# A hybrid S5 and mLSTM layer with a gated FFN: the first half of the output projection's features is summed in other PSUM banks than the second, in blocks 1 to 3

## The chip, the cores and the metric

The kernel runs on one core of one Trainium2 chip. The metric is the device time of one execution in microseconds (us), lower being better. Three runs of the kernel before took 2789.68, 2792.05 and 2795.96 us; the median is 2792.05 us. Every time below is in us unless it is marked otherwise. The engines are called as the profile calls them: PE (TensorE, matrix products), DVE (VectorE), ACT (ScalarE), POOL (GpSimd) and SP (SyncE, which issues the DMA transfers).

## The reference

One layer of a sequence model works on 16 meta tokens and 2048 tokens (L = 2064) of width 1024 in float32. The token mixer runs two branches, a state-space model (`y_a`) and a chunked mLSTM (`y_b`), gates and merges them, projects the sum with `w_out`, and adds the normed result to its input. The channel mixer is a convolutional gated FFN of width 2816. The part around the change is this:

```python
merged = (jax.nn.sigmoid(ga) * (y_a.astype(dtype) @ w_a)
          + jax.nn.sigmoid(gb) * (y_b.astype(dtype) @ w_b))
h1 = x + rmsnorm(merged @ w_out, g_post)                       # end of the token mixer

h2 = rmsnorm(h1, g_pre)                                        # channel mixer
a = causal_dwconv(h2 @ w_gate, w_conv, b_conv)
out = h1 + rmsnorm((gelu(a) * (h2 @ w_up)) @ w_down, g_post2)
```

The kernel returns the 2048 rows behind the meta tokens.

## The kernel before, in words

**How a product is made.** Every float32 operand is split in two parts, a high part (a copy in the float32r format) and a low part (what is left). A product of two matrices is then three passes of PE into one PSUM bank: high by high, high by low, low by high (`mm3`, lines 171 to 174). So each pass has its own line: L172 needs the two high parts, L173 the low part `wl` of the second operand (in the output projection, of the weights), L174 the low part of the first. Weights are split when they have landed: `split_w` (L153 to L160) lets ACT write the high part `wh` (L156) and DVE then the low part `wl` (L158, with a scale L160). The pool that holds `ws` (the weights as loaded), `wh` and `wl` is `dw`, with two buffers of each.

**PSUM.** The eight banks are three rings: `PS_BUFS = {"mm": 2, "ac": 4, "tp": 2}` (L33). `pst(tag, shape)` takes the next bank of a ring, and the first matmul into it waits until whoever read that bank last is done.

**The loop around the change.** The tokens of the mixer's last part are worked in four blocks of about 512 (four tiles of 128 rows; one block has a tile of 2 rows besides). For b = 0 to 3 the loop calls:

- `branches(b)`: for eight groups of features it multiplies both branches by their weights (results in `mm` and `ac`), DVE gates them with the loaded `gat` tiles (L978, L982, L983), and the merged sum is split into `mh` and `ml` (ACT L985, DVE L986).
- `front_a(b+1)` and `front_b(b+1)`: the first prepares the next block's state-space output without PE. The second loads the next block's mLSTM output as `yt` (L882); PE transposes it through the `tp` banks (L885), DVE gates it (L955) with a loaded `ot`, and it is split (ACT L956, DVE L957). In the last turn two `norm_block` calls stand here instead: rows of `h1` are loaded (L124), normed (ACT L135, DVE L105, POOL L107, DVE L137), transposed through `tp` (PE L148), multiplied by a gain out of the bank (DVE L150), and written to `h2` (L151), which the FFN reads.
- `out_post(b-1, i)` for the tiles of the block before: norm of the projected rows (ACT L1029, DVE L1031 and L105, POOL L107 for the power of minus one half, giving `rs`), DVE L1039 (multiply by `rs` and gain) and L1040 (add the input `xh`, loaded by L1037 into three buffers), and the write of `h1` (L1041).
- `out_proj(b)`: lines 992 to 1020, the changed function. For each half `nh` of the 1024 output features it takes one bank per token tile, loads the weights two k steps at a time (L1003; so four pairs make up a half), splits each pair, multiplies, and then copies the banks out to `o0` tiles (ACT L1016; DVE L1014 for two tiles of the very last half).
- `glu(b+1)` for the next block, in `mm`.

Behind the loop stand `ops_first(0)` (L1072: loads of `h2` by L1061, a small POOL memset at L1060, splits by ACT L1068 and DVE L1069, differences L1078 to L1080) and the FFN.

**What sets the order.** The kernel is built with a tile framework whose scheduler simulates a timeline and writes the instructions of each engine in the order in which its simulation starts them. The calls above give dependences and priorities; the order on each engine is the scheduler's. At run time each engine works through its own list in that order, and an instruction that waits holds up everything behind it on that engine. SP and POOL are such lists too.

Of the kernel before, what the change touches and what calls it, by code (L numbers as in the profile page):

```python
# [49 lines left out]
def mixer_ffn_kernel(  # L50
# [102 lines left out]
    def split_w(pl, ws, n, scale=1.0):  # L153
        wh = pl.tile([128, n], F32R, tag="wh", name="wh")
        wl = pl.tile([128, n], F32R, tag="wl", name="wl")
        S.activation(wh, ws, AF.Copy, scale=scale)  # L156
        if scale == 1.0:
            V.tensor_tensor(wl, ws, wh.bitcast(F32), ALU.subtract)  # L158
        else:
            V.scalar_tensor_tensor(wl, ws, scale, wh.bitcast(F32), ALU.mult, ALU.subtract)  # L160
        return wh, wl
# [9 lines left out]
    def mm3(ps, lh, ll, rh, rl, first, last):  # L171
        T.matmul(out=ps, lhsT=lh, rhs=rh, start=first, stop=False)  # L172
        T.matmul(out=ps, lhsT=lh, rhs=rl, start=False, stop=False)  # L173
        T.matmul(out=ps, lhsT=ll, rhs=rh, start=False, stop=last)  # L174
# [11 lines left out]
    def pst(tag, shape):  # L186
        return psp.tile(shape, F32, tag=tag, name=tag, bufs=PS_BUFS[tag])
# [378 lines left out]
    with ExitStack() as phG:  # L566
# [38 lines left out]
        b = gw.tile([68, 128], F32, name="b")  # L605
# [386 lines left out]
    def out_proj(b):  # L992
        ts, n, pieces, rowt = blkC[b]
        mh, ml = mg[b]
        os_ = {}
        for nh in range(2):
            pss = {}
            for i, (c0, rows) in enumerate(rowt):
                pss[i] = pst("mm" if rows == 2 else "ac", [rows, 512])
            for k in range(KD):  # L1000
                if k % 2 == 0:
                    ws = dw.tile([128, D], F32, tag="ws", name="ws")
                    P.dma_start(out=ws.rearrange("p (k n) -> p k n", k=2),  # L1003
                                in_=w_out[k * 128:(k + 2) * 128, nh * 512:(nh + 1) * 512].rearrange(
                                    "(k p) n -> p k n", k=2))
                    w2 = split_w(dw, ws, D)
                wh, wl = (t[:, k % 2 * 512:k % 2 * 512 + 512] for t in w2)
                for i, (c0, rows) in enumerate(rowt):
                    mm3(pss[i], mh[k // 4][:, k % 4, c0:c0 + rows], ml[k // 4][:, k % 4, c0:c0 + rows], wh, wl,
                        k == 0, k == KD - 1)  # L1010
            for i, (c0, rows) in enumerate(rowt):
                o = cp.tile([128, 512], F32, tag="o0", name="o0", bufs=OB)
                if b == 3 and nh and i % 2:
                    V.tensor_copy(o[:rows], pss[i])  # L1014
                else:
                    S.activation(o[:rows], pss[i], AF.Copy)  # L1016
                os_[i, nh] = o
                if b == 3:
                    P.dma_start(out=o3_d[i * 128:(i + 1) * 128, nh * 512:(nh + 1) * 512], in_=o)
        op[b] = os_  # L1020
# [129 lines left out]
    for b in range(4):  # L1150
        done = branches(b)
        if b < 3:
            front_a(b + 1)
            front_b(b + 1)
        else:
            for j in range(2):
                norm_block(j, Small(cr, "n", 2))
        if b:
            with tc.issue_after(done.ins):
                for f in posts(b - 1):  # L1160
                    f()
        out_proj(b)
        if b < 3:
            glu(b + 1)
# [114 lines left out]
    for m in range(NF):  # L1279
        if m:  # L1280
            wt = weights_second(*weights(m))
        if 1 <= m < 9:
            b, c0, rows = late[m - 1]
# [153 lines left out]
```

## Time and profile before

| What | Value |
|---|---|
| three runs | 2789.68, 2792.05, 2795.96 us |
| the profiled execution | 2792.36 us, its span 2790.6 us |
| mean granted clock of PE over the span | 0.998 |
| PE busy | 2759.1 us (99%) |
| DVE, ACT, POOL busy | 1761.1 us (63%), 1054.7 us (38%), 136.8 us (5%) |
| DMA queue q1 | 392.86 MB, 43.9% of the 16 DMA engines' span |

The span runs from the first to the last instruction of the profiled execution; 1.8 us of its own time lie around it. Busy shares are averages over all stages. "Idle before" in a row of the timeline is the time in which the engine had nothing to do just ahead of that instruction, with what ended it. The granted clock is the share of full speed that the throttle gave PE. `a<-b,c` names what an instruction writes and reads; for matmuls the names are those of the bank's ring and of the two operands.

### The profile page before, as it was taken

What the parts mean: (1) busy time and instruction counts of PE and PEld (TensorE: products, weight loads), DVE (VectorE), ACT (ScalarE), POOL (GpSimd) and SP (SyncE); (2) the same over time, 40 slices, a digit from 0 to 9 for tenths busy, and PEclk for the clock granted to TensorE, in tenths of its full rate; (3) what the DMA queues carried; (4) which work ended last, traced back from release to release, by engine and by line L of the source; (5) the groups of instructions that cost most, each with busy time, mean ns of one, the idle gap of its engine ahead of it and who ended that gap; (6) DMA issues with size and microseconds to landing.
All of it is one profiled execution on the core that took longest, in us unless ns stands there. A gap on an engine that the chain in (4) does not pass through costs nothing.

```text
span 2790.6 us, 40815 instructions
## 1 busy us (share of the span) xinstructions
PE 2759.1 (99%) x15590; PEld 2484.9 (89%) x15590; DVE 1761.1 (63%) x3429; ACT 1054.7 (38%) x1979; POOL 136.8 (5%) x225
## 2 busy tenths in 40 slices
PE   8999999999999999999999999999999999999999
PEld 8999999999999987777799999998788788888887
DVE  4637799377555464676798887786776683224333
ACT  6102344233444444344354434453443352224221
POOL 1000000000000000000100000000000000000000
PEclk9999999999999999999999999999999999999999
DMA  9333443212454574667744462252222244335453
GB/s 309 106 79 131 158 147 121 71 69 72 145 159 144 167 212 121 223 196 250 265 157 138 159 234 87 73 176 85 80 80 81 79 145 149 99 90 165 157 166 128
DMA packets 323478, 395.47 MB, mean 142 GB/s; under 512 B 40321, under 2 KB 229142, under 8 KB 322642
## 3 DMA queue, kind: packets, MB, share of 16 engines
q1 hardware_dynamic: 323282, 392.86, 43.9%
q8 instruction: 122, 2.00, 0.3%
q14 instruction: 74, 0.61, 0.1%
HBM read 284.47 MB, written 108.31 MB: 141 GB/s over the span
## 4 chain that ended last, share of the span: by engine, by line
PE 82%; DMA 7%; DVE 6%; ACT 1%; issue 1%; POOL 1%; SPq 0%; DVEq 0%; POOLq 0%; ACTq 0%
PE mm L172 10%; PE mm L174 10%; PE mm L173 10%; PE ac L173 9%; PE ac L174 9%; PE ac L172 8%; PE ac L179 4%; PE ac L178 4%; PE ac L177 4%; PE mm L177 3%; PE mm L179 3%; PE mm L178 3%; DMA wu<-in_w_up_dram 2%; DMA gat<-gab_d 1%; DVE w L1125 1%
## 5 line engine op out<-in xcount | busy, mean ns | idle before, releaser
L174 PE MATMUL mm<-hTh,wl 128*128 128x410 f32 (+3 forms) x1216 | 428.0, 352 | 0.0
L172 PE MATMUL mm<-hTh,wh 128*128 128x410 f32 (+3 forms) x1216 | 427.6, 352 | 0.0
L173 PE MATMUL mm<-hTl,wh 128*128 128x410 f32 (+3 forms) x1216 | 427.4, 352 | 0.0
L1339 DVE TENSOR_TENSOR yhl<-ys,yhl 128x1024 fp32r<-128x1024 f32 (+1 forms) x96 | 109.1, 1137 | 291.9 <-ACT yhl L1338 291.9
L173 PE MATMUL ac<-t,yhl 128*128 128x512 f32 x704 | 278.5, 396 | 0.0
L174 PE MATMUL ac<-t,yhl 128*128 128x512 f32 x704 | 277.3, 394 | 0.0
L172 PE MATMUL ac<-t,yhl 128*128 128x512 f32 x704 | 276.6, 393 | 0.0
L177 PE MATMUL mm<-t,w 128*128 128x258 f32 (+2 forms) x792 | 253.7, 321 | 3.5 <-DVE u L1226 2.6
L178 PE MATMUL mm<-t,w 128*128 128x258 f32 (+2 forms) x792 | 253.5, 320 | 0.4 <-DVE t L1069 0.4
L177 PE MATMUL ac<-t,w 128*128 128x258 f32 (+2 forms) x792 | 253.2, 320 | 0.6 <-ACT u L1217 0.6
L179 PE MATMUL ac<-t,w 128*128 128x258 f32 (+2 forms) x792 | 253.1, 320 | 0.1
L179 PE MATMUL mm<-t,w 128*128 128x258 f32 (+2 forms) x792 | 252.5, 320 | 0.7 <-DVE w L1125 0.7
L178 PE MATMUL ac<-t,w 128*128 128x258 f32 (+2 forms) x792 | 253.1, 320 | 0.0
L173 PEld LDWEIGHTS mm<-hTl,wh 128*128 128x128 f32 x1216 | 228.7, 188 | 2.6
L174 PEld LDWEIGHTS mm<-hTh,wl 128*128 128x128 f32 x1216 | 228.8, 188 | 2.3
L172 PEld LDWEIGHTS mm<-hTh,wh 128*128 128x128 f32 x1216 | 228.7, 188 | 2.0
L1338 ACT ACTIVATE yhl<-ys 128x1024 fp32r<-128x1024 f32 (+1 forms) x96 | 95.0, 990 | 348.4 <-PE ac L173 345.9
L156 ACT ACTIVATE wh<-ws 128x1024 fp32r<-128x1024 f32 x104 | 109.9, 1059 | 237.8 <-PE mm L173 137.5
L1124 ACT ACTIVATE w<-s 128x512 fp32r<-128x512 f32 x176 | 109.3, 628 | 164.7 <-DVE s L1139 70.3
L177 PEld LDWEIGHTS mm<-t,w 128*128 128x128 f32 x792 | 149.7, 189 | 18.0 <-DVE u L1226 4.4
L172 PEld LDWEIGHTS ac<-t,yhl 128*128 128x128 f32 x704 | 132.4, 188 | 32.3
L177 PEld LDWEIGHTS ac<-t,w 128*128 128x128 f32 x792 | 149.2, 189 | 13.0 <-ACT u L1217 1.1
(453 smaller groups left out, 6074.1 us busy)
## 6 DMA issues: line engine op xcount, KB each, us to landing
ys<-y_d SPq DMA_DIRECT2D x64, 512.0 KB, 3.7
wg<-in_w_gate_dram SPq DMA_DIRECT2D x44, 512.0 KB, 3.6
wu<-in_w_up_dram SPq DMA_DIRECT2D x44, 512.0 KB, 4.3
gab_d<-ev SPq DMA_DIRECT2D x80, 205.0 KB, 2.4
ws<-in_w_m_dram SPq DMA_DIRECT2D x32, 512.0 KB, 3.8
ws<-in_w_ba_dram SPq DMA_DIRECT2D x32, 512.0 KB, 4.0
ws<-in_w_out_dram SPq DMA_DIRECT2D x32, 512.0 KB, 5.3
gat<-gab_d SPq DMA_DIRECT2D x48, 256.0 KB, 4.8
```

What stands on the lines that cost most here:

```text
L156: S.activation(wh, ws, AF.Copy, scale=scale)
L172: T.matmul(out=ps, lhsT=lh, rhs=rh, start=first, stop=False)
L173: T.matmul(out=ps, lhsT=lh, rhs=rl, start=False, stop=False)
L174: T.matmul(out=ps, lhsT=ll, rhs=rh, start=False, stop=last)
L177: T.matmul(out=ps, lhsT=lh, rhs=rh, start=first, stop=False, skip_group_check=True)
L178: T.matmul(out=ps, lhsT=lh, rhs=rl, start=False, stop=False, skip_group_check=True)
L179: T.matmul(out=ps, lhsT=ll, rhs=rh, start=False, stop=last, skip_group_check=True)
L1124: S.activation(t[:, 0], src, AF.Copy)
L1125: V.tensor_tensor(t[:, 1], src, t[:, 0].bitcast(F32), ALU.subtract)
L1338: S.activation(yh, ys, AF.Copy)
L1339: V.tensor_tensor(yl, ys, yh.bitcast(F32), ALU.subtract)
```

## The change

In `out_proj`, a two-row tile keeps its `mm` bank and block 0 keeps `ac` for both halves. In blocks 1 to 3 the second half (`nh` = 1) keeps the four `ac` banks, and the first half takes `mm`, `mm`, `tp`, `tp` for its four tiles.

```diff
         for nh in range(2):
             pss = {}
             for i, (c0, rows) in enumerate(rowt):
-                pss[i] = pst("mm" if rows == 2 else "ac", [rows, 512])
+
+                tag = "mm" if rows == 2 else "ac" if b == 0 or nh else ("mm", "tp")[i // 2]
+                pss[i] = pst(tag, [rows, 512])
             for k in range(KD):
```

Every line behind it has a number higher by two: L1016 before is L1018 after, L1039 and L1040 are L1041 and L1042, L1069 is L1071. No instruction is added or removed, but the scheduler, which now sees other banks, writes another order on every engine in this part of the program.

PE in the first half of block 1's projection, before. `ac_11712` to `ac_11715` are the banks of the four tiles, `wh_11718` and `wl_11719` the split weights of the first pair, `11748/11749` of the second, `11778/11779` of the third; `t8` to `t11` are parts of the merged sum. The last use of the first pair stands ahead, the first need of the third pair's low part (`wl_11779`) behind; 20 more matmuls stand where rows are left out.

```order
L173 MATMUL ac_11715<-wl_11719,t8_11210 128x512
L174 MATMUL ac_11715<-wh_11718,t10_11212 128x512
L172 MATMUL ac_11715<-wh_11748,t8_11210 128x512
...
L885 MATMUL tp_12427<-ident_79,yt_12425 128x128 x4
L885 MATMUL tp_12439<-ident_79,yt_12437 128x128 x2
L172 MATMUL ac_11712<-wh_11778,t9_11211 128x512
L172 MATMUL ac_11713<-wh_11778,t9_11211 128x512
L172 MATMUL ac_11714<-wh_11778,t9_11211 128x512
L172 MATMUL ac_11715<-wh_11778,t9_11211 128x512
L885 MATMUL tp_12439<-ident_79,yt_12437 128x128 x2
L173 MATMUL ac_11712<-wl_11779,t9_11211 128x512
```

The same place after the change:

```order
L174 MATMUL tp_11715<-wh_11718,t10_11212 128x512
L172 MATMUL tp_11715<-wh_11748,t8_11210 128x512
L173 MATMUL tp_11715<-wl_11749,t8_11210 128x512
L174 MATMUL tp_11715<-wh_11748,t10_11212 128x512
L172 MATMUL tp_11715<-wh_11748,t8_11210 128x512
L173 MATMUL tp_11715<-wl_11749,t8_11210 128x512
L174 MATMUL tp_11715<-wh_11748,t10_11212 128x512
L172 MATMUL mm_11712<-wh_11778,t9_11211 128x512
L172 MATMUL mm_11713<-wh_11778,t9_11211 128x512
L172 MATMUL tp_11714<-wh_11778,t9_11211 128x512
L172 MATMUL tp_11715<-wh_11778,t9_11211 128x512
L173 MATMUL mm_11712<-wl_11779,t9_11211 128x512
```

The first two tiles (`mm`) now work through the second pair before the last tile (`tp_11715`) does the first pair's products. So the first pair's buffers, which the third pair's split needs, come free 10 matmuls ahead of the first need of `wl_11779`, where they came free 25 matmuls and eight transposes ahead of it. The transposes of the next block's `yt` (L885), which stood here, go behind this half.

DVE around the split of that third pair (`wl_11779`), before. `o0` are the projected tiles of block 0, `rs` their row factors from POOL, `xh` their loaded inputs:

```order
L955 SCALAR_TENSOR_TENSOR ot_11595<-ot_11595,tp_11599 128x512
L955 SCALAR_TENSOR_TENSOR ot_12411<-ot_12411,tp_12415 128x512
...
L1039 SCALAR_TENSOR_TENSOR o0_10955<-o0_10955,rs_11616,g2b_9936 2x512
L1039 SCALAR_TENSOR_TENSOR o0_11114<-o0_11114,rs_11616,g2b_9936 2x512
L105 TENSOR_SCALAR ms_11635<-sq_11633 128x1
L1040 TENSOR_TENSOR o0_10955<-o0_10955,xh_11618 2x512
L158 TENSOR_TENSOR wl_11779<-ws_11776,wh_11778 128x1024
L1040 TENSOR_TENSOR o0_11114<-o0_11114,xh_11623 2x512
L1039 SCALAR_TENSOR_TENSOR o0_10957<-o0_10957,rs_11637,g2b_9936 128x512
```

The same place after:

```order
L1041 SCALAR_TENSOR_TENSOR o0_10955<-o0_10955,rs_11616,g2b_9936 2x512
L1041 SCALAR_TENSOR_TENSOR o0_11114<-o0_11114,rs_11616,g2b_9936 2x512
L105 TENSOR_SCALAR ms_11635<-sq_11633 128x1
L1042 TENSOR_TENSOR o0_10955<-o0_10955,xh_11618 2x512
L1042 TENSOR_TENSOR o0_11114<-o0_11114,xh_11623 2x512
L1041 SCALAR_TENSOR_TENSOR o0_10957<-o0_10957,rs_11637,g2b_9936 128x512
L1041 SCALAR_TENSOR_TENSOR o0_11116<-o0_11116,rs_11637,g2b_9936 128x512
L105 TENSOR_SCALAR ms_11656<-sq_11654 128x1
L1042 TENSOR_TENSOR o0_10957<-o0_10957,xh_11639 128x512
L158 TENSOR_TENSOR wl_11779<-ws_11776,wh_11778 128x1024
L1042 TENSOR_TENSOR o0_11116<-o0_11116,xh_11644 128x512
```

The split now stands behind the second addition to the 2-row tile, both multiplications of the first 128-row tile and its first addition; of the two gatings ahead of it the second (`ot_12411`) has gone behind. In block 2 the same shape is found around `wl_12610`: before it stands behind the first addition to the first tile, after behind the first addition to the second tile.

DVE in block 3 between the splits of the second and the third pair (`wl_13534`, `wl_13564`), before; left out are two merges, four sums and a split for the FFN:

```order
L158 TENSOR_TENSOR wl_13534<-ws_13531,wh_13533 128x1024
L983 TENSOR_TENSOR gat_13183<-gat_13183 128x512
...
L1079 TENSOR_TENSOR mk_13794<-mk_13799,mk_13794 128x2x514
L105 TENSOR_SCALAR ms_13420<-sq_13418 128x1
L158 TENSOR_TENSOR wl_13564<-ws_13561,wh_13563 128x1024
L1080 TENSOR_TENSOR mk_13799<-mk_13799,mk_13794 128x2x514
L1039 SCALAR_TENSOR_TENSOR o0_12667<-o0_12667,rs_13422,g2b_9936 128x512
L1039 SCALAR_TENSOR_TENSOR o0_12799<-o0_12799,rs_13422,g2b_9936 128x512
```

and after, where the left-out rows are a merge and four sums first, then more of the same norm work:

```order
L158 TENSOR_TENSOR wl_13534<-ws_13531,wh_13533 128x1024
...
L150 TENSOR_TENSOR mk_13391<-tp_13406,g3_87 128x512
L105 TENSOR_SCALAR ms_13420<-sq_13418 128x1
L1041 SCALAR_TENSOR_TENSOR o0_12667<-o0_12667,rs_13422,g2b_9936 128x512
...
L1042 TENSOR_TENSOR o0_12669<-o0_12669,xh_13445 128x512
L1041 SCALAR_TENSOR_TENSOR o0_12671<-o0_12671,rs_13464,g2b_9936 128x512
L1041 SCALAR_TENSOR_TENSOR o0_12803<-o0_12803,rs_13464,g2b_9936 128x512
L105 TENSOR_SCALAR ms_13483<-sq_13481 128x1
L158 TENSOR_TENSOR wl_13564<-ws_13561,wh_13563 128x1024
L158 TENSOR_TENSOR wl_13594<-ws_13591,wh_13593 128x1024
```

The third split now stands behind the norm work of three tiles of block 2, and the fourth pair's split (`wl_13594`) directly behind it. The `norm_block` work (`mk_13391<-tp_13406` is its last row) was all done before this projection in the old order, since its transposes use the `tp` banks ahead of the projection's tiles; the first steps of `ops_first` (`mk_13777` and so on) went with it, from `branches(3)` to a place behind `wl_13594`.

POOL in the same stretch, before. `rs_13422` to `rs_13485` are the row factors that DVE's L1039 waits for; the memsets belong to `ops_first`:

```order
L1060 MEMSET mk_13777 128x2x2
L1060 MEMSET mk_13782 128x2x2
L1060 MEMSET mk_13794 128x2x2
L1060 MEMSET mk_13799 128x2x2
L1060 MEMSET mk_13866 128x2x2
L107 TENSOR_TENSOR rs_13422<-ms_13420,neghalf_84 128x1
L107 TENSOR_TENSOR rs_13443<-ms_13441,neghalf_84 128x1
L1060 MEMSET mk_13869 128x2x2
L107 TENSOR_TENSOR rs_13464<-ms_13462,neghalf_84 128x1
L1060 MEMSET mk_13881 128x2x2
L107 TENSOR_TENSOR rs_13485<-ms_13483,neghalf_84 128x1
L1060 MEMSET mk_13884 128x2x2
```

and after:

```order
L1062 MEMSET mk_13777 128x2x2
L1062 MEMSET mk_13782 128x2x2
L107 TENSOR_TENSOR rs_13422<-ms_13420,neghalf_84 128x1
L107 TENSOR_TENSOR rs_13443<-ms_13441,neghalf_84 128x1
L1062 MEMSET mk_13794 128x2x2
L107 TENSOR_TENSOR rs_13464<-ms_13462,neghalf_84 128x1
L107 TENSOR_TENSOR rs_13485<-ms_13483,neghalf_84 128x1
L1062 MEMSET mk_13799 128x2x2
L1062 MEMSET mk_13866 128x2x2
```

Two memsets now stand directly ahead of `rs_13422`, and a third one ahead of `rs_13464`; each takes over a buffer of the `mk` ring from a `norm_block` tile, whose write to `h2` must have landed first.

## The prediction

> **What bounds the kernel now.** I read the page first, then the waits of PE in the stretch that holds the four blocks, then the timelines of PE, DVE, ACT and POOL where PE waited. The page says that PE is the bound over the whole span:
>
> ```profile
> span 2790.6 us, 40815 instructions
> PE 2759.1 (99%) x15590; PEld 2484.9 (89%) x15590; DVE 1761.1 (63%) x3429; ACT 1054.7 (38%) x1979; POOL 136.8 (5%) x225
> ```
>
> PE does the same matmuls before and after, so the change can only move the time in which PE waits or runs at a lower clock. The waits of PE from 950 to 1420 us are these (us in total, times, longest):
>
> ```profile
> PE ac L173 <- DVE wl L158: 5.0, 5, 2.9
> PE tp L885 <- DMA yt<-yb_d: 2.9, 3, 1.2
> PE ac L172 <- ACT o L1016: 2.0, 1, 2.0
> PE ac L174 <- DVE wl L160: 0.8, 1, 0.8
> PE ac L172 <- ACT wh L156: 0.5, 1, 0.5
> ```
>
> Only the third row, once 2.0 us, is a wait for a PSUM bank. The first, the largest, is a wait for the split of projection weights on DVE. The bank wait on PE, and what ACT did meanwhile:
>
> ```profile
> 1241.30 0.85 PE L172 MATMUL ac<-wh,t 128*128 128x512 f32 x3
> ...
> 1255.39 0.50 PE L173 MATMUL ac<-wl,t 128*128 128x512 f32 x1 [0.53 <-DVE wl L158]
> ...
> 1266.72 0.50 PE L173 MATMUL ac<-wl,t 128*128 128x512 f32 x1 [0.24 <-DVE wl L158]
> ...
> 1271.57 0.50 PE L172 MATMUL ac<-wh,t 128*128 128x512 f32 x1 [2.03 <-ACT o L1016]
> 1271.91 0.40 PE L173 MATMUL ac<-wl,t 128*128 128x512 f32 x1
> 1272.14 0.39 PE L174 MATMUL ac<-wh,t 128*128 128x512 f32 x1
> ...
> 1273.49 0.63 PE L173 MATMUL ac<-wl,t 128*128 128x512 f32 x1
> 1273.92 0.63 PE L174 MATMUL ac<-wh,t 128*128 128x512 f32 x1
> ```
> ```profile
> 1263.77 1.30 ACT L1016 ACTIVATE o<-ac 128x512 f32<-128x512 f32 x2 [1.91 <-PE ac L174]
> ...
> 1269.88 1.06 ACT L135 ACTIVATE mk<-mk 128x1024 f32<-128x1024 f32 x1 [4.21 <-DMA mk<-h_d]
> ...
> 1270.94 1.07 ACT L1016 ACTIVATE o<-ac 128x512 f32<-128x512 f32 x2
> ```
>
> ACT copied two banks out, then stood 4.21 us at the norm of a block whose rows had not landed, and copied the other two only behind it; PE's second half needed them. Starts lie 0.23 us apart ahead (1271.91 to 1272.14), and 0.43 us apart (1273.49 to 1273.92) a little behind the wait: the granted clock fell for about eight matmuls, 8 x 0.20 = 1.6 us. I call this the slow clock. It follows the other long wait too, in block 3's projection:
>
> ```profile
> 1374.85 0.50 PE L173 MATMUL ac<-wl,t 128*128 128x512 f32 x1 [2.95 <-DVE wl L158]
> ...
> 1376.22 0.63 PE L173 MATMUL ac<-wl,t 128*128 128x512 f32 x1
> ```
>
> So these two waits cost 2.03 + 1.6 = 3.6 and 2.95 + 1.6 = 4.6 us.
>
> **Block 2's bank wait.** With the first half in `mm` and `tp`, the second half's `ac` banks were last read in `branches`, long done. The 2.03 us and their slow clock go: -3.6. The first half's banks are wanted next by `glu` and by the next transposes, which in the new order stand at least 36 matmuls (8 us) behind that half's end; ACT's four copies take 1.30 + 1.07 us, so this costs nothing unless ACT is held as in the row at 1269.88, and then no more than the 3.6 of now. What is late next is the weight split.
>
> **The split of the third weight pair, block 1.** This is the term that speaks against the change. In the order before, PE needs `wl` of the third pair after 48 matmuls of two pairs, 4 of L172 and 8 transposes. The rows, and DVE ahead of that split:
>
> ```profile
> 1133.72 0.86 PE L172 MATMUL ac<-wh,t 128*128 128x512 f32 x3
> ...
> 1148.03 0.50 PE L173 MATMUL ac<-wl,t 128*128 128x512 f32 x1 [1.06 <-DVE wl L158]
> ...
> 1154.61 0.63 PE L885 MATMUL tp<-ident,yt 128*128 128x128 f32 x4 [0.78 <-DMA yt<-yb_d]
> ```
> ```profile
> 1141.83 0.69 DVE L955 SCALAR_TENSOR_TENSOR ot<-ot,tp 128x512 f32<-128x512 f32 x1 [0.78 <-DMA ot<-o_d]
> ...
> 1144.59 0.16 DVE L1031 TENSOR_TENSOR sq<-ssq 128x1 f32<-128x1 f32 x1 [0.53 <-ACT jk L1029]
> 1144.78 1.40 DVE L1039 SCALAR_TENSOR_TENSOR o<-o,rs,g2b 2x512 f32<-2x512 f32 x2
> 1146.11 0.13 DVE L105 TENSOR_SCALAR ms<-sq 128x1 f32<-128x1 f32 x1
> 1146.17 0.67 DVE L1040 TENSOR_TENSOR o<-o,xh 2x512 f32<-2x512 f32 x1
> 1146.77 1.21 DVE L158 TENSOR_TENSOR wl<-ws,wh 128x1024 fp32r<-128x1024 f32 x1
> ```
>
> After, the transposes are gone from here, so PE is there 52 x 0.231 = 12.0 us behind the half's start: 1133.72 + 12.0 = 1145.7. DVE does the split behind three more steps: the other L1040 of the 2-row tile (0.6 start to start, 1146.17 to 1146.77), the L1039 pair of the first full tile (1.33, 1144.78 to 1146.11) and its L1040 (0.6), with a look at POOL's factor in between (about 0.4). That is +2.9. One L955 with its wait no longer stands ahead (0.78 + 0.6 = 1.4 us), but DVE waited for ACT's square at 1144.59 all the same, and does again if that step doesn't move. So the split ends at 1146.77 + 1.2 + 2.9 = 1150.9 less 0 to 1.4: a wait of 3.8 to 5.2 us. Even with DVE idle the split can't be early: its buffers come free 10 matmuls (2.3 us) ahead of the need, and `wh` (1.06, as another 128x1024 step of ACT, the L135 above) and `wl` (1.2) fill that. I take 4.0, near the lower end of the two, since ACT and DVE lose a wait for a load ahead of it; for the range the ends are 0.5 and 5.2. Queued behind the waiting PE is only the rest of the projection; ACT, DVE and SP run on. Old wait off: 4.0 - 1.06 = +2.9. Slow clock: +1.6. The transposes' waits for `yt` go, since that load is needed half a projection later: -0.78 here and -0.96 for an earlier one of the same kind:
>
> ```profile
> 1099.56 0.63 PE L885 MATMUL tp<-ident,yt 128*128 128x128 f32 x4 [0.96 <-DMA yt<-yb_d]
> ```
>
> Block 1: 2.9 + 1.6 - 1.7 = **+2.8**.
>
> **The `tp` banks of the first half.** In block 1 the last tile's bank must have been read by the next block's gating (L955). That step ended at 1141.83 - 0.78 = 1141.05 (first row of DVE above), 7.3 behind the half's start; the tile's first matmul stands 36 matmuls in, 8.3 us. One us is to spare: I cost it at nothing, and every us that L955 is later than that is one us of waiting.
>
> **Block 2.** The same shape; the split stood directly behind the first L1040 and now stands behind one more L1040, the next L1039 pair and its L1040, with a wait for POOL between:
>
> ```profile
> 1252.12 1.42 DVE L1039 SCALAR_TENSOR_TENSOR o<-o,rs,g2b 128x512 f32<-128x512 f32 x2 [0.66 <-POOL rs L107]
> ...
> 1254.11 1.22 DVE L158 TENSOR_TENSOR wl<-ws,wh 128x1024 fp32r<-128x1024 f32 x1
> 1255.24 0.69 DVE L1040 TENSOR_TENSOR o<-o,xh 128x512 f32<-128x512 f32 x1
> 1256.38 1.41 DVE L1039 SCALAR_TENSOR_TENSOR o<-o,rs,g2b 128x512 f32<-128x512 f32 x2 [0.44 <-POOL rs L107]
> ```
>
> That is 0.6 + 0.44 + 1.33 + 0.6 = +3.0; one L150 (0.6) no longer stands ahead. The split's end goes from 1255.3 to 1257.7. PE, without 12 transposes, needs it at 1241.30 + 12.0 = 1253.3: a wait of up to 4.4. I take 3.0 (ends 0.5 and 4.4): the steps are counted, and the wait of 0.66 us at the start of the chain may be shorter when less of the norm work is in flight. So 3.0 - 0.53 + 1.6 for the slow clock, -0.24 for the old second wait, -3.6 for the bank: **+0.2**.
>
> **Block 3.** Here two queues change besides. Gone are the 2.95 us with their slow clock, since the fourth pair's split now follows the third's directly, and two waits in `branches(3)`, whose splits stand in another order (0.5 and 0.8 in the list of waits): -5.9. Added is first the third pair's split. Between it and the second pair's stand a merge and an L150 (128x512 like L1040, 0.6 each), three L1039 pairs (4.0), three L1040 (1.8) and eight small steps (0.06 like L105): 7.5, and 3 x 0.5 for POOL: 9.0. But POOL's first factor is now behind a memset that waits for the write of a norm tile to `h2`, which leaves after the L150 at about the projection's start. Such writes take this long (us to landing):
>
> ```profile
> h_d<-mk SPq DMA_DIRECT2D x8, 512.0 KB, 6.6
> mk<-h_d SPq DMA_DIRECT2D x8, 1026.0 KB, 4.9
> ws<-in_w_out_dram SPq DMA_DIRECT2D x16, 512.0 KB, 7.7
> ```
>
> So the factor is there at about start + 0.3 + 6.6 + 0.8 = 7.7; from it the norm work of three tiles (4.0 + 1.8 and two waits for POOL of 0.5, the small steps in between: 6.9) puts the split's start at 14.6 and its end at 15.8; PE needs it at 12.0 + 0.6 (four transposes) = 12.6. A wait of 3.2 (ends: 0.5 if the write lands early enough not to matter, 6 if the third factor, which has a memset of its own ahead, is late as well), and 1.6 of slow clock. Then the second half: its first split stands behind nine large steps for the FFN, of which seven stood in `branches(3)` before, and they need loads of `h2` that leave when the last norm tile's write has landed: 4.8 + 6.6 = 11.4, landed at 16.3, and the next two, which share the DMA engines, at about 20. A large step takes 1.14 start to start:
>
> ```profile
> 1361.03 1.22 DVE L1079 TENSOR_TENSOR mk<-mk 128x1028 f32<-128x1028 f32 x1
> 1362.17 0.15 DVE L105 TENSOR_SCALAR ms<-sq 128x1 f32<-128x1 f32 x1
> ```
>
> From 17, where the fourth split ends, one L1039 pair (1.3), nine large steps (10.3) and four L1040 (2.4) end at 31, the split at 32.1. PE needs it at 22.2 (96 matmuls) + 0.6 + 4.8 + 0.9 = 28.5: 3.6 (ends 0 and 5) and 1.6 of slow clock. The sum: 3.2 + 1.6 + 3.6 + 1.6 - 5.9 = **+4.1**.
>
> In all +2.8 + 0.2 + 4.1 = **+7.1**. The profiled execution took 2792.36 us, 0.3 above the median of three: 2792.36 + 7.1 = **2799.5**. What a measurement of this kernel can tell from no change is about 0.2%, 5.6 us, so this is slower by little more than that.
>
> **The rivals.** *Faster:* DVE does not come late. If ACT's squares and with them the whole norm work move up with the splits, every third pair is ready within 12 us of the half's start, and only what goes is left: bank wait -3.6, `yt` -1.7, block 3's -4.6: 2792.36 - 9.9 = 2782.5. For it: DVE is busy 63% of the span, and a scheduler that plans with times put it so. Against: in the trace DVE already comes late to the splits, with less ahead of them. It decides at the split's end: 12 us behind the start of the half. *No difference:* the new waits are there but near 2 us each. Four such waits (8.0), less the old ones in the same places (1.06 + 0.53) and all that goes (3.6 + 0.24 + 1.7 + 5.9 = 11.4), give -5.0 with no slow clock: 2787.4; with it (4 x 1.6) 2793.8. I put this at 2791. By the Trainium skill, "TensorE: Matmul & The Clock Gate", section "Why this matters for your kernels", PE should have no gaps over about 3 us between bursts, one idle window being what halves the clock; by that rule waits of 2 us would cost no slow clock, and this case would stand at its lower end. The trace doesn't bear it out: the clock fell behind a wait of 2.03 us. *Much slower:* block 3 takes in three more loads of 1026 KB, where the DMA engines are already busy:
>
> ```profile
> 1351.00:1403.60 52.60, 49.45 (x207) 39.42 (x206) 39.39 (x55) 20.06 (x24) 9.44 (x8) 0.97 0.74 258
> ```
>
> At 0.74 busy for 258 GB/s (last two columns) the engines are full at 350, so 3.1 MB more are 8.8 us of transfer, and the stretch comes to 317. Then loads are late, the third split of the second half waits too, and the FFN's first operands come behind it: 9 more, 2809. Against: a tenth of the engines' time stays free. That the banks don't change is excluded by the order of PE, which shows `mm` and `tp`.
>
> **How the numbers follow.** Chances: forecast 0.46 (2795 to 2804), faster 0.21, no difference 0.21, much slower 0.12. Of the forecast's case about a third lies below 2797.6, where a difference can be told from the median. Faster: 0.21 and a little from the no-difference case, less as much of its own: 0.22. Same: 0.21 + 0.15, about 0.35. Slower: 0.31 + 0.12 = 0.43. The range reaches down to the faster rival's middle and up past the much slower one's: 2783 to 2811.
>
> **What would show it.** In the trace after: no wait of PE for L1018 in blocks 1 to 3; three waits for DVE `wl` L158 of 3 to 4 us at the third pair of the first half, and one at the first pair of the second half of block 3, each with half-speed rows behind it; POOL's first factor of block 3 behind a memset that a DMA released. I am wrong if PE finds the third pair ready, or if PE waits for a `tp` or `mm` bank instead.

## The result, and the profile after

| | Before | After |
|---|---|---|
| median (lowest to highest) of five runs | 2795.22 us (2789.68 to 2797.62) | 2821.87 us (2816.53 to 2823.29) |
| the profiled execution, its span | 2792.36 us, 2790.6 us | 2822.39 us, 2820.6 us |
| mean granted clock of PE | 0.998 | 0.996 |

The ratio is 1.0096, with a 95% interval of 1.0085 to 1.0107: 26.7 us slower. Forecast were 2799.5 us and a range up to 2811; the sign was right, the size was not. The two profiled spans differ by 30.0 us, and the page of after shows the same instructions, with longer busy times of PE (2759.1 us before) and POOL (136.8 us before):

```profile
span 2820.6 us, 40816 instructions
...
PE 2772.2 (98%) x15590; PEld 2488.0 (88%) x15590; DVE 1760.4 (62%) x3429; ACT 1052.8 (37%) x1979; POOL 152.6 (5%) x225
```

To find the 30 us I cut both spans at the first instruction of the same stage on PE. A block's stage runs from the start of its projection to the start of the next one.

| Stage | before | after | more | forecast |
|---|---|---|---|---|
| everything ahead of block 0's projection | 1019.17 | 1020.30 | +1.1 | 0 |
| block 0 | 114.55 | 114.57 | 0.0 | 0 |
| block 1 | 107.58 | 107.83 | +0.3 | +2.8 |
| block 2 | 112.85 | 113.91 | +1.1 | +0.2 |
| block 3's projection | 49.65 | 58.20 | +8.6 | +4.1 |
| FFN, first pass | 449.60 | 451.26 | +1.7 | 0 |
| FFN, second pass | 433.93 | 451.23 | +17.3 | 0 |
| down projection | 496.01 | 496.07 | +0.1 | 0 |

So the changed blocks cost 9.9 us, not far from the 7.1 that were forecast, though by two misses that partly cancel (1.4 for 3.0 in blocks 1 and 2, 8.6 for 4.1 in block 3), and more than half of the loss lies in the FFN's second pass, which begins half a millisecond behind the changed code. Each figure is from one trace. In the five kernels here that have the old banks in every block, block 1 takes 106.7 to 110.1 us, block 2 112.6 to 113.3, block 3's projection 49.3 to 50.5 and the first pass 448.9 to 453.7, so a difference of 1 or 2 us in one of these stages says little. The rows of the table by stage for these two places (us, busy us and instructions of PE, PEld, DVE, ACT and POOL, granted clock, busy share of the DMA engines, GB/s), before:

```profile
1354.15:1403.80 49.65, 46.50 (x193) 37.05 (x192) 36.66 (x53) 19.19 (x23) 9.44 (x8) 0.97 0.75 263
...
1853.40:2287.33 433.93, 431.52 (x1874) 348.52 (x1873) 314.85 (x502) 183.74 (x299) 30.77 (x23) 1.00 0.30 97
```

and after:

```profile
1356.61:1414.81 58.20, 49.98 (x199) 39.23 (x198) 45.92 (x61) 21.53 (x27) 6.02 (x10) 0.91 0.82 296
...
1866.07:2317.30 451.23, 438.98 (x1875) 346.70 (x1873) 314.24 (x501) 182.74 (x297) 49.04 (x22) 1.00 0.29 94
```

In the second pass the counts are the same to one or two and the clock is full. POOL is busier, 49.0 us for 30.8 with one instruction fewer, and so is PE, 439.0 for 431.5 with the same matmuls.

**The blocks.** The waits of PE from 950 to 1420 us, the view that the prediction started from (us in total, times, longest):

```profile
PE mm L173 <- DVE wl L158: 8.6, 4, 2.9
PE ac L172 <- ACT wh L156: 5.6, 1, 5.6
PE mm L172 <- ACT wh L156: 1.7, 3, 1.0
PE tp L885 <- DMA yt<-yb_d: 1.1, 1, 1.1
```

No row waits for L1018 any more, the copies out of a bank: the bank wait is gone as forecast. In its place stand the third pair's `wl` in each block, and, not forecast, a wait of 5.6 us for ACT's `wh`. The timeline of PE at these waits:

```profile
1150.06 0.79 PE L173 MATMUL mm<-wl,t 128*128 128x512 f32 x1 [2.94 <-DVE wl L158]
1150.65 0.63 PE L174 MATMUL mm<-wh,t 128*128 128x512 f32 x1
...
1152.78 0.60 PE L173 MATMUL tp<-wl,t 128*128 128x512 f32 x1
1153.21 0.40 PE L174 MATMUL tp<-wh,t 128*128 128x512 f32 x1
...
1258.74 0.57 PE L173 MATMUL mm<-wl,t 128*128 128x512 f32 x1 [2.67 <-DVE wl L158]
...
1371.53 0.69 PE L173 MATMUL mm<-wl,t 128*128 128x512 f32 x1 [2.13 <-DVE wl L158]
...
1389.08 2.07 PE L172 MATMUL ac<-wh,t 128*128 128x512 f32 x4 [5.56 <-ACT wh L156]
1391.69 0.80 PE L173 MATMUL ac<-wl,t 128*128 128x512 f32 x1 [0.53 <-DVE wl L158]
```

Behind each of the waits of 2.1 us and more the matmuls start 0.43 us apart (1150.65 to 1153.21 is six of them in 2.56 us) and then again 0.23 us apart. ACT ahead of the long wait at 1389:

```profile
1382.23 1.06 ACT L1070 ACTIVATE t<-mk 128x1028 fp32r<-128x1028 f32 x1 [7.12 <-DVE mk L1081]
1383.20 1.07 ACT L1018 ACTIVATE o<-mm 128x512 f32<-128x512 f32 x2
1384.15 2.01 ACT L1070 ACTIVATE t<-mk 128x1028 fp32r<-128x1028 f32 x2
...
1387.95 2.02 ACT L156 ACTIVATE wh<-ws 128x1024 fp32r<-128x1024 f32 x2
```

ACT stood 7.12 us for a difference that DVE makes for the FFN (L1081), then wrote FFN operands (L1070) and copied banks out, and only behind these the second half's first `wh`.

**The FFN's second pass.** It works through 22 units. In each, DVE makes one `s4` (L1192 before, L1194 after), which is the last use of that unit's `wg` tile; the next unit's `wg` can be loaded only behind it. The view of that one line gives its count, durations, and the first and the last start. Before:

```profile
L1192 DVE TENSOR_TENSOR s<-wg,s x22: 680/684/698, 1860.9 to 2273.2; 128x512 f32<-128x512 f32 x22
```

and after:

```profile
L1194 DVE TENSOR_TENSOR s<-wg,s x22: 679/682/686, 1873.4 to 2308.0; 128x512 f32<-128x512 f32 x22
```

A unit took 412.3 / 21 = 19.6 us before and takes 434.6 / 21 = 20.7 after. PE's own work in a unit is about 433.93 / 22 = 19.7 us, as it hardly waited before. So after, the period is no longer PE's but that of a closed chain. It is followed best in one unit, on DVE first (start, us; idle before and its releaser):

```profile
2077.17 0.68 DVE L1194 TENSOR_TENSOR s<-wg,s 128x512 f32<-128x512 f32 x1
2082.10 0.69 DVE L1127 TENSOR_TENSOR w<-wg,w 128x512 fp32r<-128x512 f32 x1 [4.25 <-ACT w L1126]
...
2083.31 0.68 DVE L1127 TENSOR_TENSOR w<-wu,w 128x512 fp32r<-128x512 f32 x1
...
2088.30 0.69 DVE L1140 TENSOR_TENSOR s<-wu 128x512 f32<-128x512 f32 x1 [1.91 <-DMA wu<-in_w_up_dram]
...
2090.78 0.75 DVE L1258 SCALAR_TENSOR_TENSOR cc<-gp,cwf,cc 128x512 f32<-128x512 f32 x1
2091.45 0.68 DVE L1127 TENSOR_TENSOR w<-wg,w 128x512 fp32r<-128x512 f32 x1
2092.05 1.29 DVE L1127 TENSOR_TENSOR w<-s,w 128x512 fp32r<-128x512 f32 x2
2093.25 0.69 DVE L1263 TENSOR_TENSOR cc<-cc,u 128x512 f32<-128x512 f32 x1
2094.87 0.75 DVE L1258 SCALAR_TENSOR_TENSOR cc<-gp,cwf,cc 128x512 f32<-128x512 f32 x1 [0.93 <-ACT cc L1256]
...
2098.00 0.68 DVE L1194 TENSOR_TENSOR s<-wg,s 128x512 f32<-128x512 f32 x1
```

POOL and ACT in the same unit:

```profile
2091.68 2.30 POOL L1202 COPY gp<-halo 128x2 f32<-128x2 f32 x1 [18.53 <-ACT w L1126]
```
```profile
2081.44 0.63 ACT L1126 ACTIVATE w<-wg 128x512 fp32r<-128x512 f32 x1 [4.71 <-DMA wg<-in_w_gate_dram]
...
2094.02 0.82 ACT L1256 ACTIVATE cc<-gp,cbf,cwf 128x512 f32<-128x512 f32 x1 [0.85 <-POOL gp L1202]
```

The chain: `s4` at 2077.17 frees `wg`; the next `wg` has landed at 2081.44 and ACT splits it; DVE's split of `wu` (2083.31) frees the other buffer, and the next `wu` is there at 2088.30. In DVE's list the two steps of the convolution that read the old `gp` stand behind that wait, the last at 2090.78. Then POOL may write the carried columns (the halo) into the next `gp` (2091.68, until 2093.98), ACT starts the convolution from it (2094.02), DVE continues it (2094.87), and the next `s4` stands behind that, at 2098.00: 20.83 us. In the order before, some units have the same form, and some have their `s4` ahead of that part, as DVE shows in two units in a row:

```profile
2076.51 0.68 DVE L1192 TENSOR_TENSOR s<-wg,s 128x512 f32<-128x512 f32 x1
...
2096.85 0.69 DVE L1192 TENSOR_TENSOR s<-wg,s 128x512 f32<-128x512 f32 x1
...
2113.61 0.69 DVE L1261 TENSOR_TENSOR cc<-cc,u 128x512 f32<-128x512 f32 x1
2114.21 0.69 DVE L1192 TENSOR_TENSOR s<-wg,s 128x512 f32<-128x512 f32 x1
2114.81 0.75 DVE L1256 SCALAR_TENSOR_TENSOR cc<-gp,cwf,cc 128x512 f32<-128x512 f32 x1
```

The first of the two has the long form and takes 20.3 us (2076.51 to 2096.85). In the second the `s4` at 2114.21 stands ahead of the convolution's step at 2114.81, and it takes 17.4. Such short units make up for the long ones. After the change all units from the fifth on take 20.5 us or more. The 21 periods grew by 22.3 us and the pass by 17.3, since the last `s4` stood 14.1 us ahead of the pass's end before and 9.3 after; I read these 4.8 us as operands that were prepared ahead.

### The profile page after: what moved, and what is told of

Same layout as the page of the kernel before. It is cut to its first block, busy times and chain, and to the rows that moved or that the text cites. A ratio compares the mean times of both kernels' runs of the same rounds, so it can differ in the third digit from the quotient of the medians.

```text
span 2820.6 us, 40816 instructions
## 1 busy us (share of the span) xinstructions
PE 2772.2 (98%) x15590; PEld 2488.0 (88%) x15590; DVE 1760.4 (62%) x3429; ACT 1052.8 (37%) x1979; POOL 152.6 (5%) x225
## 5 line engine op out<-in xcount | busy, mean ns | idle before, releaser
L177 PEld LDWEIGHTS mm<-t,w 128*128 128x128 f32 x792 | 149.8, 189 | 26.7 <-ACT w L1126 11.0
```

Source lines behind the costliest of these rows:

```text
L177: T.matmul(out=ps, lhsT=lh, rhs=rh, start=first, stop=False, skip_group_check=True)
```

## The experiments

The theories. **Order theory:** the second pass is slow only because the scheduler, whose simulated times the new banks shift, writes another order from the turn between the passes on. **Banks rival:** it is the new banks that slow it, whatever the order. **Loop theory:** the chain above, through POOL's halo copy, sets the period. **Norm theory:** block 3's projection is dear because the norm transposes, which also need `tp`, are pushed behind block 2's use of it.

**Other order, old banks.** In the kernel before, two calls at the turn change places; the scheduler then writes the second pass just as in after.

```diff
-    op_again(4, op1, (t4(10), t4(11)))
     op_again(3, op1, (q4(0), q4(1)))
+    op_again(4, op1, (t4(10), t4(11)))
```

> The banks of the kernel before (ac for both halves); only the two calls that load the operands of products 4 and 3 at the start of the FFN's second pass are swapped, upon which the scheduler writes the units of that pass in the same order as in the changed kernel. Theory (order): the 17.3 us that the second pass lost (433.9 to 451.2 us from its first product to the down projection) come from that order alone, so this kernel loses them with the old banks: second pass about 450 us, blocks as before, in all about +17 us, 2810. Rival (banks): the loss follows the new banks at run time, so this kernel takes 2792 to 2796 and its second pass 434.

Measured: 2813.45 us, ratio 1.0069 (1.0054 to 1.0084) to a median of 2794.07. Its second pass:

```profile
1857.13:2309.00 451.87, 439.15 (x1875) 346.65 (x1873) 314.14 (x501) 182.15 (x297) 50.20 (x22) 1.00 0.29 94
```

Not one bank is changed, block 3's projection takes 49.5 us as before, and the pass takes 451.9 us as in after. The banks rival falls.

**New banks, old order; and old banks with the same edit.** In `turn()` the first weights of the second pass are called for behind the four operands rather than ahead of them; with this the scheduler writes the old pattern for both kinds of banks. The edit was made in the kernel after (first) and in the one before (second).

```diff
-        nxt.append(weights(0))
         for i, n in enumerate((1, 6, 2, 7)):
             op_again(n, op1, (t4(2 * i), t4(2 * i + 1)))
+        nxt.append(weights(0))
```

> The changed banks; only the turn between the FFN's passes loads its operands ahead of the next weights, upon which the scheduler writes the units of the second pass in the order of the kernel before. Theory (order): the second pass is back at 434 to 436 us, the blocks keep their 10 us, so the time is about 2804, +10 to +12 against the kernel before. Rival (banks): second pass 451, time about 2820.

> Control for the run before: old banks with the same edit of the turn, so that the FFN's second pass has the same order as there. Theory (order): equal to the kernel before within 4 us, second pass 434 to 436 us; the difference to the run with the new banks, about 10 us, is then the cost of the banks in blocks 1 to 3 alone. Rival (banks): the same time here, but 25 us between the two.

Measured: with the new banks 2804.44 us, 1.0031 (1.002 to 1.0042); with the old ones 2794.65 us, 1.0002 (0.9992 to 1.0012). The second pass of the first of the two:

```profile
1860.63:2293.90 433.27, 431.48 (x1874) 348.57 (x1873) 315.43 (x503) 184.56 (x302) 30.29 (x23) 1.00 0.30 99
```

The pass is back at 433.3 us (434.4 in the other). So the banks by themselves cost 2804.44 - 2794.65 = 9.8 us, and what is left to 2821.87, about 17, is the order. The 9.8 is a difference of medians: the nine times with the new banks reach from 2797.42 to 2808.10 us, and the trace is that of one of the lower ones (2798.95). In it the four blocks take 389.8 us, against 383.2 with the old banks. Block 3's projection still takes 57.5 us here, 49.3 with the old banks.

**The chain shortened.** The first of these kernels (old banks, other order), with POOL's copy of the halo replaced by a memset, which leaves out the carry of two columns into the second pass.

```diff
-            G.tensor_copy(gp_[:, 2:4], halo[:, m])
+            G.memset(gp_[:, 2:4], 0.0)
```

> The first kernel of these (old banks, the slow order of the FFN's second pass), but POOL's copy of the halo into gp (2.3 us) is a memset (0.1 us), so the convolution of the second pass starts without the last two columns of the first: that carry is left out. The order of ACT and DVE stays the same. Theory (loop): in that order each unit is a closed chain of about 20.8 us (load of wg, its split, the split of wu that stands behind it, load of wu, sums on DVE, the convolution step that waits for POOL, and back to the last use of wg), longer than PE's 19.5, and POOL's copy is a link of it; 2.2 us less make it 18.6, PE is the bound again, and the second pass falls from 452 to 430 to 436 us. Rival (the order is slow for another reason, for example PE waiting for its splits on a crowded ACT or DVE): second pass within 4 us of 452.

Measured: 2796.5 us, 1.0009 (0.9999 to 1.0019), second pass 435.9 us in place of 451.9. POOL in it:

```profile
2097.63 0.10 POOL L1200 MEMSET gp<- 128x2 f32 x1 [19.64 <-DVE cc L1256]
```

Two microseconds less in one link, and nearly all units take 19.5 to 20.1 us in the same order: the chain without that link is 20.8 - 2.2 = 18.6, and PE's 19.7 bounds again. The loop theory holds: the copy is a link of the chain that sets the period. The other links are read from the rows above and were not shortened one by one.

**New banks in one block alone.** The kernel with new banks and old order, with them kept in block 3 only, and in block 2 only:

```diff
-                tag = "mm" if rows == 2 else "ac" if b == 0 or nh else ("mm", "tp")[i // 2]
+                tag = "mm" if rows == 2 else "ac" if b != 3 or nh else ("mm", "tp")[i // 2]
```

> The second kernel with the new banks in block 3 alone (old banks in blocks 1 and 2, old order of the FFN's second pass). Theory (norm): block 3's projection takes 8 us more (49.3 to 57.5) because new banks in the blocks before it push the transposes of the two norm_block calls, and with them the first steps for the FFN, into it; with block 3 alone they stay early, and its projection takes 49 to 52 us, blocks 1 and 2 as before (106.7 and 112.6). Rival (own banks): the 8 us follow block 3's own banks, and its projection takes 56 to 58.

> The same with the new banks in block 2 alone. Theory (norm): the norm transposes are pushed behind block 2's first half, and block 3's projection, though in its old banks, takes 53 to 58 us against 49.3; block 2 (112.6) is within 1.5 us, block 1 as before (106.7). Rival (own banks): block 3's projection 49 to 50.

Measured in one run each: 2791.48 us with block 3 only, its projection 48.8 us; 2798.54 us with block 2 only, block 3's projection 53.2 us although its own banks are the old ones, and a wait of 4.43 us for ACT in the FFN's first unit:

```profile
1409.28 0.58 PE L177 MATMUL mm<-t,w 128*128 128x258 f32 x1 [4.43 <-ACT w L1126]
```

With block 2 only, blocks 1 and 2 took 103.3 and 109.7 us, about 3 us less each than with the old banks (106.7 and 112.6), which was not expected. So its four blocks together took no longer than there (383.0 against 383.2 us), and what it lost came in the first pass (457.7 us, against 448.9 to 453.7 with the old banks). The line of the norm's transposes (`norm_block`, L148) from 1290 to 1425 us, with the first and the last start, in before:

```profile
L148 PE MATMUL tp<-ident,mk x22: 270/273/275, 1294.7 to 1311.9; 128*128 128x128 f32 x22
```

in after:

```profile
L148 PE MATMUL tp<-ident,mk x64: 270/272/276, 1295.1 to 1360.3; 128*128 128x128 f32 x64
```

with the new banks in block 3 only:

```profile
L148 PE MATMUL tp<-ident,mk x22: 270/273/275, 1294.5 to 1311.7; 128*128 128x128 f32 x22
```

and in block 2 only:

```profile
L148 PE MATMUL tp<-ident,mk x62: 270/272/276, 1291.3 to 1354.4; 128*128 128x128 f32 x62
```

Where block 2 holds `tp` banks through its first half, about 40 transposes of the norms that stood ahead of 1290 us now fall in the time up to block 3's projection or into its first 4 us, and with them the writes of `h2` and the FFN's first operands, which then fill ACT and DVE in the projection's middle. The norm theory holds in kind, but it explains only a part of the price: of the 8.2 us by which block 3's projection is longer with all the new banks (57.5 against 49.3), block 2's banks alone bring 3.9 and block 3's own none. The other 4.3 come only with the new banks in more than one block, and no run here takes them apart.

**`mm, mm, ac, ac`.** New banks and old order, but the first half of blocks 1 to 3 takes no `tp` bank:

```diff
-                tag = "mm" if rows == 2 else "ac" if b == 0 or nh else ("mm", "tp")[i // 2]
+                tag = "mm" if rows == 2 or (b and nh == 0 and i < 2) else "ac"
```

> The second kernel (old order of the FFN's second pass), but the first half of blocks 1 to 3 takes the banks mm, mm, ac, ac: no tp. Theory (norm): what cost block 3 its 8 us was that the projection's first half held the tp banks, which the norm transposes need. Without tp they stay early, block 3's projection takes 46 to 50 us (57.5 with tp, 49.3 with the old banks), the splits stand early enough in blocks 1 and 2, and the time is 2786 to 2793. Rival (any bank beside ac moves the splits and the FFN's first steps): block 3's projection 54 us or more, time 2799 to 2806.

Measured: 2796.55 us, 1.0012 (1.0001 to 1.0022). Block 3's projection fell to 49.9 us as the norm theory has it (20 transposes in that window), but the time that I expected did not come: block 2's stage took 115.5 us, with a wait of 3.36 us for `wh` in `branches(3)`, at 1318.55.

**The third split ahead of the norm work.** New banks and old order; the projection is called first, and the norm work of the block before is let out only behind the third pair's `wl` (`lows` collects the splits):

```diff
+        at = len(lows)
+        out_proj(b)
         if b:
-            with tc.issue_after(done.ins):
+            with tc.issue_after(lows[at + 2].ins):
                 for f in posts(b - 1):
                     f()
-        out_proj(b)
```

> As the second kernel (new banks, old order of the second pass), but the norm work of the block before is issued behind the split of the projection's third weight pair on DVE. Theory (late splits): the waits for that split (2.9, 2.7 and 2.1 us) and the slow clock behind each (about 1.5) go; block 3's wait of 5.6 us at the second half may stay. So 8 to 12 us less than the second kernel, about 2793. Rival (the banks make PE wait as such, whatever DVE does, or the buffers of the weights come free too late for any order): the waits stay at 2 us or more, and the time is within 3 us of the second kernel's.

Measured: 2803.78 us, 1.0034 (1.0021 to 1.0047): a miss. The waits at which it was aimed went (block 1's stage 103.5 us, block 3's projection 50.9), but others came: one of 2.31 us for `wl` of block 3's fourth pair, three of 1.7 to 2.0 us at the FFN's first products (first pass 459.4 us), and one in `branches(3)`, which made block 2's stage 119.0 us (line numbers here are two higher, so L158 is ACT's `wh`):

```profile
1317.60 0.80 PE L174 MATMUL mm<-t,wh 128*128 128x512 f32 x1 [5.59 <-ACT wh L158]
```

**A buffer of its own for `wu`.** In the FFN `wg` and `wu` share a ring of two buffers. Here `wu` has its own from the second unit on (`up` is the pool that holds it), in the kernel before:

```diff
-        wu = dw.tile([128, D], F32, tag="ws", name="wu")
+        wu = (up or dw).tile([128, D], F32, tag="wu" if up else "ws", name="wu")
```

> The kernel before (old banks), but the up weights wu of the FFN's units are loaded into a buffer of their own instead of sharing two with the gate weights wg, so that wg can be loaded a unit earlier. The scheduler writes another order of the second pass. Theory (loop): the load of wg leaves the chain of a unit, the chain is 4 us shorter, and PE is the bound in both passes: second pass 430 to 433 us, the time 0 to 4 us below the kernel before. Rival: the order written for it has a loop of its own as long as PE's 19.5 us a unit, and the time is 5 us or more above the kernel before.

Measured: 2793.12 us, 0.9993 (0.9984 to 1.0003), second pass 431.7 us: 2 us less than before there, and no difference in all that can be told.

**That buffer with new banks.** These three runs have the buffer of its own for `wu`, the turn as in before and after, and three choices of banks: `mm, mm, ac, ac` in blocks 1 to 3; the change in block 3 only; the change in blocks 1 and 3. The last one's line:

```diff
+                tag = "mm" if rows == 2 else "ac" if b in (0, 2) or nh else ("mm", "tp")[i // 2]
```

> The same banks (mm, mm, ac, ac; ac) together with the buffer of its own for wu in the FFN, in place of the edit of the turn. Theory: the gains add: second pass 431 to 432 us (434 before), blocks 2 to 8 us less than before, so 2784 to 2790 against 2794. Rival: blocks as before, and the time within 0.2% of the kernel before.

> New banks (mm, mm, tp, tp in the first half) in block 3 alone, and the buffer of its own for wu. Theory: the two parts that cost nothing or gained by themselves (block 3's projection 48.8 against 49.5 us, second pass 431.7 against 434) add: 2789 to 2792 against 2794. Rival: the order shifts elsewhere in the blocks and eats it, 2794 to 2798.

> The same with the new banks in blocks 1 and 3. Theory (norm): block 2 keeps its old banks, so the norm transposes still have tp banks in time and block 3's projection stays at 49 to 51 us; block 1 adds nothing or a gain of 1 us: 2788 to 2792. Rival: block 1's tp banks delay the chain as block 2's do, block 3's projection 53 us or more, time over 2796.

Measured: 2797.35 us, 1.0015 (1.0006 to 1.0024); 2792.94 us, 1.0001 (0.9992 to 1.001); 2804.32 us, 1.0038 (1.0026 to 1.0051). The second pass takes 431.7 or 431.8 us in all three, so the order of the turn does no harm in them, and block 3's projection takes 50.2, 48.9 and 50.8 us. The first did not bring the gain that I expected, the second stands just above its expected range and level with the kernel before, and in the third block 3's projection came as the theory has it and the time as its rival has it. The first and the third lose it in block 2's stage (118.1 and 118.9 us). PE in the third:

```profile
1272.39 0.80 PE L172 MATMUL ac<-wh,t 128*128 128x512 f32 x1 [3.04 <-ACT o L1018]
...
1326.45 0.80 PE L172 MATMUL mm<-t,wh 128*128 128x512 f32 x1 [2.96 <-ACT wh L156]
```

Block 2's bank wait, left as it was, has grown from 2.03 to 3.04 us, and `branches(3)` waits for its weights again. No version beat the kernel before by what can be measured.

## Why the prediction was right or wrong

**The step that failed** is the sum, "In all +2.8 + 0.2 + 4.1", as the whole of the change: it took every stage behind block 3's projection at nothing, without a row for it. The scheduler decides the order of the whole program in one simulated timeline, and with the new banks it also wrote another order of the FFN's second pass, +17.3 us of the 30.0, where a closed chain of 20.8 us a unit bounds and no longer PE's 19.7. Shown for this: the same pass, with the old banks, in that order (451.9 us), and with the new banks in the old order (433.3 us). The rows of the order that the prediction rests on end at block 3, though the order differs in the second pass too. The price could have been bounded from the trace of before: a unit of the long form took 20.3 us there already, against 19.7 of PE; 20 such units would be 12 us.

**The bank wait:** right. No wait for L1018 is left in blocks 1 to 3; no PE row shows a wait for an `mm` or `tp` bank.

**The third pair's split:** right in kind, a little too dear. Waits of 2.94, 2.67 and 2.13 us for DVE `wl`, where 4.0, 3.0 and 3.2 were forecast, each with its slow clock (seven steps of 0.43 in place of 0.23 us behind the first, 1.4 us, where 1.6 stood). That each brought one was in part luck: with the same order of the blocks (new banks, old order of the second pass) the same split was waited for 1.88 us in block 1 and 2.19 in block 2, and the clock stayed full. Blocks 1 and 2 together came to +1.4 where +3.0 was forecast. They are better taken together, since 20 PE instructions of block 1's stage moved to block 2's (the counts by stage are 450 and 502 after, 470 and 481 before).

**The `yt` waits of block 1:** half right. Both went, but in the place of the earlier one came waits of 0.98 and 0.27 us for ACT's `wh`, which took back 1.3 of the 1.7.

**Block 3:** its first half as described. The factor came behind a memset that a write of `h2` released, as POOL shows:

```profile
1362.43 0.10 POOL L1062 MEMSET mk<- 128x4 f32 x1 [11.21 <-DMA h_d<-mk]
1362.64 0.55 POOL L107 TENSOR_TENSOR rs<-ms,neghalf 128x1 f32<-128x1 f32 x1
```

It was there 6.6 us behind the projection's start (1363.19 less 1356.61), not 7.7, so the split's wait was 2.13 and not 3.2. The second half is the term that was mis-sized: 3.6 for DVE's `wl` and 1.6 of slow clock were forecast. PE waited 5.56 for ACT's `wh` and 0.53 for `wl`, and needed 6.19 us from 1389.08 to 1395.27 for 12 matmuls of 0.23, which less the wait of 0.53 is a slow clock of 2.9 us: 9.0 in place of 5.2. I had followed DVE's list with the FFN's splits in it and not ACT's, where the same splits stand ahead of `wh`. The later norm work, from which this comes, was put down to block 3's own `tp` tiles; the two runs with one block's banks show that block 3's own bring none of it and block 2's alone about half (3.9 of 8.2 us).

**The much slower rival** had the right direction, and its place, the FFN's beginning, was the wrong one: the first pass grew by 1.7 us. That is less than its spread among these kernels: it took 453.7 us with old banks and the other order, 449.2 with new banks and the old.

**Left open:** why the simulated timeline tips at the turn; what makes the first pass vary; the 1.1 us ahead of block 0, where one stretch of slow clock stands at about 732 us, in code that the change does not touch; the 4.3 us of block 3's projection that come only with the new banks in more than one block; and why `branches(3)` comes to wait for `wh` in four of the variants.

## What to carry to other kernels

Where a scheduler writes the order from a simulated timeline, a small edit can change the order far behind it: compare the order of the whole program on every engine, loop by loop, before the sum of a change is closed. A loop whose closed chain through several engines is nearly as long as the bound engine's own work is fragile, here 20.3 of a unit's long form against 19.7 of PE; its length is worth working out from one unit of the trace, whatever the change. And a buffer ring that another stage uses too (here `tp`) moves that stage's work, so that the price of taking it can fall due in the next block.

## What the runs showed of the hardware

A copy of 128x2 elements took POOL 2.30 us in the unit followed above. The grouped rows of POOL in the second pass (count, busy us, mean ns) before and after:

```profile
L1200 POOL COPY gp<-halo 128x2 f32<-128x2 f32 x22 | 25.5, 1159 | 389.7 <-DVE cc L1256 212.7 <-ACT w L1124 177.0
```
```profile
L1202 POOL COPY gp<-halo 128x2 f32<-128x2 f32 x22 | 44.4, 2019 | 389.4 <-ACT w L1126 189.5 <-DVE cc L1258 186.0 <-ACT t L1330 13.9
```

The same copy takes 2.02 us on average in one order and 1.16 in the other, and the memset in its place 0.10. It took 0.18 us where DVE was idle (after, at 1905.27) and 0.19 beside a DVE sum that reads a PSUM bank (before, at 1956.64). In the unit shown it began at 2091.68, while DVE ran three splits and a product of two SBUF tiles without a gap (2091.45 to 2093.94), and it ended at 2093.98, as soon as DVE paused. The Trainium skill, "SBUF — State Buffer", section "SBUF: two separate sides", says that DVE and POOL share a pair of ports as an exclusive lock, which a DVE instruction with two SBUF inputs holds against a POOL instruction that reads SBUF; the copy reads SBUF and the memset does not, and the rows agree with it. What lets a waiting copy in is not shown: in the order before, the copy at 2091.14 ended 0.05 us behind the third such DVE step, although the next split (2092.70) follows there without idle time in the profile.

The granted clock fell behind waits of 2.03, 2.13, 2.67, 2.94 and 5.56 us, each of the short ones costing 1.4 to 1.6 us more by it. But the length of a short wait does not decide this. With the new banks and the old order, PE waited 2.19 us in block 2, and the matmuls behind it start 0.23 us apart:

```profile
1257.56 0.50 PE L173 MATMUL mm<-wl,t 128*128 128x512 f32 x1 [2.19 <-DVE wl L158]
```

With the old banks and the same edit of the turn, a wait of 2.84 us at 1373.19 left the clock of block 3's projection at 1.00, where before, behind one of 2.95, it was 0.97:

```profile
1352.60:1401.92 49.32, 45.24 (x193) 35.81 (x192) 36.55 (x53) 19.06 (x23) 10.04 (x8) 1.00 0.75 265
```

With the new banks in block 2 alone, a wait of 1.86 us at 1100.19 brought the slow clock. Behind every wait above 3 us in the blocks of these runs it came. So 1.6 us of slow clock is what a wait of 2 to 3 us may cost here, not what it always costs, and what decides it these runs do not show. The rule of the Trainium skill, "TensorE: Matmul & The Clock Gate", section "Why this matters for your kernels", that was weighed in the prediction puts the limit at gaps of about 3 us; here waits of 1.9 to 2.9 us brought the loss in some executions and not in others.
